# Gate matrices by one float32r matmul of 256 columns, and the entry to the second block by half features without GpSimd

## Chip, cores and metric

One core of a Trainium2 chip runs the kernel. The metric is device time in microseconds, the median of the timed runs. The engines are TensorE (PE; its weight loads are the row PEld), VectorE (DVE), ScalarE (ACT), GpSimd (POOL) and SyncE (SP), which issues most transfers.

## The reference

256 tokens of 1024 features pass two blocks. The first has a mixer (retention and differential attention) and then a retrieval feed-forward layer, the part that the change touches first:

```python
def peer_ffn(h, w_query, sub_keys, expert_u, expert_v):
    ...
        q = (hb @ w_query).reshape(t, PEER_HEADS, 2, PEER_HALF)
        s = jnp.einsum('thpc,hpnc->thpn', q, sub_keys).astype(jnp.float32)
        v1, i1 = lax.top_k(s[:, :, 0], PEER_TOPK)
        v2, i2 = lax.top_k(s[:, :, 1], PEER_TOPK)
        ...
        best, pos = lax.top_k(cand, PEER_TOPK)
        experts = jnp.take_along_axis(cand_idx, pos, axis=-1)
        gate = jax.nn.softmax(best, axis=-1).astype(hb.dtype)
        act = jax.nn.gelu(jnp.einsum('thkd,td->thk', u, hb), approximate=False)
        return jnp.einsum('thk,thkd->td', gate * act, vsel)
```

Eight heads pick 16 of 128 x 128 experts for each token. The second block has two layers. Each ends in attention to 256 memory tokens and a gated feed-forward layer; the first begins with a short convolution, the second with causal attention (`moba`) on rotated queries and keys:

```python
def short_conv_mixer(h, w_in, w_conv, w_out):
    b_gate, c_gate, u = jnp.split(h @ w_in, 3, axis=-1)
    z = c_gate * u
    conv = lax.conv_general_dilated(
    ...
    return (b_gate * conv) @ w_out
```

Everything is float32.

## The kernel before

**Weights.** A weight block of 128 x 1024 comes from memory into `raw` (three buffers). ScalarE rounds it to float32r (`whi`, three buffers), and VectorE or GpSimd, by `lo_plan`, subtracts to get the rest (`wlo`, two buffers). `block` multiplies it in three passes of eight matmuls of 256 columns: `whi` by the high part of the activations, `wlo` by the high part, `whi` by the low part.

**The expert layer** treats all experts densely. Each of 128 weight blocks of `peer_u` makes one chunk of 128 experts for 256 tokens, and `slots` holds [128, chunk, token]. The gate of a token is a 128 x 128 matrix, made by one matmul of two one-hot matrices over the 128 chosen (head, rank) pairs: `ohA` marks the second index, `ohB` the first one and holds the gate as its value. `group` does this for four tokens, and `hot` makes the one-hots two tokens at a time. From block 32 on a table spreads the 64 groups over the remaining 94 blocks (after one block, then after two, and so on), so a group meets chunks that are already there (`done` of them, which it multiplies on the spot) and others that are yet to come (it stores the gate, and the later gelu multiplies it in). The same tokens of successive chunks lie 1 KB apart in `slots`.

```python
                    for i in range(2):
                        nc.tensor.matmul(o[:, 2 * j + i], A[:, i], Bt[:, i], start=True, stop=True)
                sl = slots[:, :, ts].rearrange("p c t -> p t c")
                if done:
                    nc.vector.tensor_mul(sl[:, :, :done], o[:, :, :done], sl[:, :, :done])
                if done < NCH:
                    nc.scalar.copy(sl[:, :, done:], o[:, :, done:])
```

Then 128 blocks of `peer_v` multiply `slots` into two accumulators `acc[th]`, one for each half of the tokens; `product` adds a chunk to one, `collect` copies one out, transposes it and adds it to the residual `x`.

**The entry to the second block.** `conv_mixer` scales `x` into the parts `hh` and `hl`, squares and adds its eight feature slices (`track`: `accsq`, `acc`) for the norm, and runs eight steps `m`, each with a pair of blocks `o` (the inputs to z) and one block `b`. The results wait in PSUM for the norm `nr`; `gate` then makes z, convolves it, and multiplies by `b` into `ct`. PSUM has two tiles `sc` (for `o` of the first two steps) and three tiles `mm`. At step 1 a hook loads the keys and values of the first memory attention (`kvt`), which ScalarE rounds and GpSimd subtracts. Steps of the second memory's projection (`fill`, with `memx`, `hmh`, `hml`) are interleaved by the table `PLACES`.

A scheduler at build time fixes the order of each engine's queue.

Of the kernel before, what the change touches and what calls it, by code (L numbers as in the profile page):

```python
# [15 lines left out]
F32 = mybir.dt.float32  # L16
# [24 lines left out]
PLACES = {0: 1, 3: 1, 5: 2, 6: 1, 10: 1, 12: 1, 's': 2, 'h': 4, 'g': 10, 'n': 1, ('g', 0): 1, 'v': 4, ('d', 1): 1, ('o', 0): 3, ('o', 2): 1, ('o', 3): 1, ('o', 4): 1, ('o', 5): 4, ('o', 7): 10, ('c', 1): 1, ('c', 3): 1, ('c', 5): 1, 'ce': 1, 'm0': 1, 'mq0': 1, 'me0': 1, 'f0': 1, 'b': 2, 'bk': 1, 'bq': 1, ('mh0', 2): 1, ('bh', 0): 1, ('bh', 5): 1, ('bh', 7): 1}  # L41
# [5 lines left out]
GPLAN = "p"  # L47
HOT = 4
QSTEPS, USTEPS = 2, 4
HOOK = 1  # L50
# [6 lines left out]
CADD = 'vector'  # L57
MIXLO = 'v'
RETLO = 'v'
AHEAD = 3  # L60
# [11 lines left out]
class Build:  # L72
    def __init__(self, ctx, tc, io):
        self.ctx, self.tc, self.nc, self.io = ctx, tc, tc.nc, io
        self.const = ctx.enter_context(tc.tile_pool(name="const", bufs=1))
        self.wpool = ctx.enter_context(tc.tile_pool(name="weights", bufs=2))
        self.psfill = ctx.enter_context(tc.tile_pool(name="psfill", bufs=1, space=PSUM))
        self.lo_turn = 0
        self.folding = []
        self.filler = self.steady = iter(())  # L80
        self.rate, self.due = RATE, 0
        self.adder = self.nc.gpsimd
        self.lo_plan = "v"
# [628 lines left out]
    def peer(self):  # L712
        nc, io = self.nc, self.io
        with ExitStack() as ctx:
# [4 lines left out]
            h = self.placed(pool, "h2h", 48), self.placed(pool, "h2l", 48)  # L719
# [16 lines left out]
            selT = gpool.tile([P, 3, T], F32, name="selT")  # L736
# [215 lines left out]
            def product(c, th, a, b, w):  # L952
                tsl = slice(th * P, th * P + P)
                for s, (x, wt) in enumerate(((a, w[0]), (b, w[0]), (a, w[1]))):
                    for dh in range(2):
# [3 lines left out]
            def collect(th):  # L959

                tsl = slice(th * P, th * P + P)
                for q in range(4):
                    e = nc.scalar.copy if th or q % 2 else nc.vector.tensor_copy
                    e(ot[:, th, q * T:(q + 1) * T], acc[th][:, q // 2, q % 2 * T:q % 2 * T + T])
                for q in range(2):
                    tr = self.psum([P, 4, P])
                    for i in range(4):
                        k = 4 * q + i
                        nc.tensor.transpose(tr[:, i], ot[:, th, k * P:(k + 1) * P], self.ident)
                    for i in range(4):  # L970
                        k = 4 * q + i
                        nc.vector.scalar_tensor_tensor(self.x[:, k, tsl], tr[:, i], gate[:, k:k + 1],
                                                       self.x[:, k, tsl], op0=OP.mult, op1=OP.add)
# [12 lines left out]
            for c, parts in ends:  # L986
                product(c, 0, *parts)
            product(ends[0][0], 1, *ends[0][1])
            collect(0)
            product(ends[1][0], 1, *ends[1][1])  # L990
            collect(1)


    def mem_kv(self, pool, mpool, l, key, value, norm=None):
# [17 lines left out]
        for m2 in range(4):  # L1012
            o = self.psum([P, 2, T], "fill")
            for i in range(2):
                self.block(o[:, i], io["mem_wk"][l, 2 * m2 + i], hm, lo=FILL_LO, late=m2 == i == 0,
# [7 lines left out]
                if i == 1:  # L1023
# [4 lines left out]
                                      lambda n, i, o: value(n, o, rn), FILL_LO)  # L1028
# [47 lines left out]
    def mem_load(self, pool, l):  # L1076
# [3 lines left out]
        def load():  # L1080
            for n in range(4):
                for part in range(2):
# [5 lines left out]
                    nc.gpsimd.tensor_sub(lo, t, hi)  # L1088

        return (kT, v), load  # L1090

    def mem_fill(self, pool, mpool, l):
# [3 lines left out]
        def key(n, o, r):  # L1096
            t = mpool.tile([P, 2, T], F32, name="kvt", tag="kvt", bufs=1)
            hi, lo = (x[:, 2 * n:2 * n + 2] for x in kT)
            self.key_out(t, o, r)
            nc.scalar.copy(hi, t)  # L1100
            nc.gpsimd.tensor_sub(lo, t, hi)
# [125 lines left out]
    def conv_mixer(self, hook):  # L1227
        nc, io = self.nc, self.io
        with ExitStack() as ctx:
# [5 lines left out]
            def gate(m, o, b):  # L1235
                cu = pool.tile([P, 2, T], F32, name="cu", tag="cu", bufs=2)
# [9 lines left out]
                nc.gpsimd.tensor_mul(y, y, r)  # L1246
# [5 lines left out]
            self.adder = getattr(nc, CADD)  # L1252
            for k in range(KC):
                self.track(self.x[:, k], k)
            self.adder = nc.gpsimd
            for m in range(KC):
                self.at(("c", m))
                if m == HOOK:
                    hook()
                o = self.psum([P, 2, T], "sc" if m < 2 else "mm")  # L1260
                for i, c in enumerate((1, 2)):
                    self.block(o[:, i], io["conv_wi"][8 * c + m], h, late=m == i == 0)
                    if m == 1 and i == NORM1:
                        r = self.tracked_norm(pool, "nr", tables=True)
                b = self.psum([P, T])
# [78 lines left out]
    def moba(self):  # L1344
        nc, io = self.nc, self.io
        with ExitStack() as ctx:
            pool = self.pool(ctx, "moba")
            mask = self.load(pool, "causal", [P, 2, T])
            hk = self.gained(pool, self.x, G_KV)
            v = pool.tile([P, 2, 1024], F32, name="v")  # L1350
# [5 lines left out]
            def value(n, i, o):  # L1356
# [3 lines left out]
                if n == 1:  # L1360
                    rn = self.by_partition(pool, r, "aux")
                waiting.append((n, o))
# [8 lines left out]
            def plain(block, h, scale):  # L1371
                o = self.psum([P, T])
                self.block(o, block, h)
                t = pool.tile([P, T], F32, name="qkt", tag="qkt", bufs=3)
                nc.vector.scalar_tensor_tensor(t, o, scale, r, op0=OP.mult, op1=OP.mult)
                return t

            def rope(out, t):
                self.rope_out(pool, t, out, self.pcos, self.psin)
# [4 lines left out]
            hq = [self.placed(pool, "hq" + c, 32) for c in "hl"]  # L1384

            def query(hd):
                return plain(io["moba_wq"][hd], hq, 128.0 ** -0.5)
# [5 lines left out]
            for hd in range(KC):  # L1393
                t = plain(io["w_k"][hd], hk, 1.0)
# [3 lines left out]
                self.gain_chunk(self.x[:, hd], G_MIX + 1, hd, hq[0][:, hd], hq[1][:, hd])  # L1398
# [224 lines left out]
```

## Time and profile before

| | before |
|---|---|
| median of 3 runs | 1889.74 us (1888.1 to 1890.78) |
| profiled execution | 1882.41 us |
| its span in the trace | 1880.6 us |
| granted TensorE clock, mean | 0.992 |
| TensorE busy | 1833.2 us, 97% |
| VectorE, ScalarE, GpSimd busy | 1313.8, 975.1, 453.7 us |

The profiled execution is 1.8 us longer than its span and is one execution; sums in the text are made against it. Busy shares are averages over all stages, and matmuls overlap, so a stage has to be read by itself.

### The profile page before, as it was taken

How to read it: one execution, taken by the hardware profiler on the slowest of the kernel's cores; microseconds unless marked ns; L12 is line 12 of the kernel's file. 1: busy time of each engine (PE TensorE's matmuls, PEld its weight loads, DVE VectorE, ACT ScalarE, POOL GpSimd, SP SyncE). 2: the span in 40 equal slices, each digit the busy share in tenths (PEclk: the TensorE clock that was granted, in tenths of full speed). 3: DMA queues.
4: the chain of work that ended last, by engine and by line, in shares of the span. 5: the costliest groups of instructions: out<-in, count | busy, mean ns of one | idle time of the engine just before them, and what ended most of it. 6: DMA issues, size and time to landing. Idle time of an engine off the chain costs nothing.

```text
span 1880.6 us, 34809 instructions
## 1 busy us (share of the span) xinstructions
PE 1833.2 (97%) x13562; PEld 1717.2 (91%) x13562; DVE 1313.8 (70%) x2592; ACT 975.1 (52%) x1533; POOL 453.7 (24%) x254
## 2 busy tenths in 40 slices
PE   8999999999999999999999998999999999999997
PEld 6796888999999999788888878999999999999997
DVE  7879875995566676865555568777765679766654
ACT  7746335445555444445545555465554645555543
POOL 0001105787766777100000004112000111110001
PEclk9999999999999999999999999999999999999999
DMA  8763444454444444755555555544555553445553
GB/s 298 254 217 105 142 129 156 170 189 169 150 160 154 157 157 157 247 191 195 195 191 193 196 192 184 191 169 148 200 193 196 190 180 124 169 136 190 187 184 124
DMA packets 99765, 335.13 MB, mean 178 GB/s; under 512 B 12400, under 2 KB 13456, under 8 KB 99216
## 3 DMA queue, kind: packets, MB, share of 16 engines
q1 hardware_dynamic: 98160, 330.68, 51.0%
q8 instruction: 106, 1.74, 0.4%
q10 hardware_dynamic: 1440, 2.23, 0.3%
q14 instruction: 59, 0.48, 0.1%
HBM read 329.59 MB, written 3.28 MB: 177 GB/s over the span
## 4 chain that ended last, share of the span: by engine, by line
PE 87%; DVE 6%; DMA 3%; ACT 3%; issue 1%; POOL 0%; SPq 0%; DVEq 0%; ACTq 0%; POOLq 0%
PE mm L144 54%; PE pair L956 17%; PE mm L179 4%; PE pair L893 3%; PE fill L179 2%; DVE wlo L122 2%; PE fill L144 1%; PE sc L144 1%; DMA mraw<-w_mod 1%; PE aux L144 1%; DMA raw<-w_mod 1%; ACT whi L118 1%; DMA raw<-peer_v 0%; PE sc L628 0%; PE sc L554 0%
## 5 line engine op out<-in xcount | busy, mean ns | idle before, releaser
L118 ACT CAST whi<-raw 128x1024 fp32r<-128x1024 f32 x564 | 591.9, 1051 | 558.3 <-PE mm L144 280.4
L122 DVE TENSOR_TENSOR wlo<-raw,whi 128x1024 fp32r<-128x1024 f32 x420 | 526.7, 1255 | 298.7 <-PE pair L956 131.6
L122 POOL TENSOR_TENSOR wlo<-raw,whi 128x1024 fp32r<-128x1024 f32 x144 | 344.7, 2395 | 131.6 <-PE mm L144 113.6
L144 PE MATMUL mm<-hh,whi 128*128 128x256 f32 (+1 forms) x1184 | 178.2, 287 | 5.9 <-DVE ct L1248 5.1
L144 PE MATMUL mm<-hl,whi 128*128 128x256 f32 (+1 forms) x1184 | 174.5, 284 | 2.1 <-DVE hl L261 1.2
L144 PE MATMUL mm<-hh,wlo 128*128 128x256 f32 (+1 forms) x1184 | 175.9, 285 | 0.0
L144 PE MATMUL mm<-h2h,whi 128*128 128x256 f32 x1152 | 168.2, 289 | 4.1 <-ACT h2h L260 4.0
L226 POOL TENSOR_TENSOR acc<-acc,accsq 128x256 f32<-128x256 f32 x42 | 42.1, 1004 | 523.1 <-ACT accsq L224 523.1
L144 PEld LDWEIGHTS mm<-hh,whi 128*128 128x128 f32 x1184 | 155.4, 190 | 10.9 <-issue 7.6
L956 PE MATMUL pair<-whi,actl 128*128 128x512 f32 x512 | 158.6, 391 | 2.4 <-DVE actl L949 2.3
L956 PE MATMUL pair<-whi,acth 128*128 128x512 f32 x512 | 158.3, 390 | 0.3 <-ACT acth L948 0.2
L956 PE MATMUL pair<-wlo,acth 128*128 128x512 f32 x512 | 157.8, 389 | 0.7 <-DVE wlo L122 0.7
L144 PEld LDWEIGHTS mm<-hl,whi 128*128 128x128 f32 x1184 | 153.5, 189 | 5.0 <-DVE hl L261 1.7
L144 PEld LDWEIGHTS mm<-hh,wlo 128*128 128x128 f32 x1184 | 154.6, 190 | 3.5 <-issue 1.5
L144 PE MATMUL mm<-h2h,wlo 128*128 128x256 f32 x1152 | 157.5, 279 | 0.0
L144 PE MATMUL mm<-h2l,whi 128*128 128x256 f32 x1152 | 157.1, 279 | 0.0
L144 PEld LDWEIGHTS mm<-h2h,whi 128*128 128x128 f32 x1152 | 147.4, 192 | 5.0 <-ACT h2h L260 4.8
L144 PEld LDWEIGHTS mm<-h2h,wlo 128*128 128x128 f32 x1152 | 144.6, 189 | 0.0
L144 PEld LDWEIGHTS mm<-h2l,whi 128*128 128x128 f32 x1152 | 144.0, 189 | 0.0
L956 PEld LDWEIGHTS pair<-whi,actl 128*128 128x128 f32 x512 | 95.4, 188 | 24.4 <-DVE actl L949 5.0
L956 PEld LDWEIGHTS pair<-wlo,acth 128*128 128x128 f32 x512 | 96.0, 188 | 21.3 <-DVE wlo L122 1.1
L956 PEld LDWEIGHTS pair<-whi,acth 128*128 128x128 f32 x512 | 95.5, 188 | 20.9 <-ACT acth L948 1.5
(407 smaller groups left out, 3062.7 us busy)
## 6 DMA issues: line engine op xcount, KB each, us to landing
raw<-peer_u SPq DMA_DIRECT2D x128, 512.0 KB, 3.5
raw<-peer_v SPq DMA_DIRECT2D x128, 512.0 KB, 3.5
raw<-ffn_gu SPq DMA_DIRECT2D x88, 512.0 KB, 4.3
raw<-ffn_dn SPq DMA_DIRECT2D x44, 512.0 KB, 3.9
raw<-w_mod SPq DMA_DIRECT2D x64, 256.0 KB, 3.8
raw<-conv_wi SPq DMA_DIRECT2D x24, 512.0 KB, 3.5
raw<-mem_wk SPq DMA_DIRECT2D x16, 512.0 KB, 4.5
mraw<-w_mod SPq DMA_DIRECT2D x16, 512.0 KB, 6.2
```

Source lines behind the costliest of these rows:

```text
L118: self.hi_copy = nc.scalar.copy(hi, raw)
L122: (nc.vector if plan == "v" else nc.gpsimd).tensor_sub(lo, raw, hi)
L144: self.matmul = nc.tensor.matmul(out, a, b, start=first and j == 0, stop=last and j == 3 * n - 1)
L179: self.matmul = nc.tensor.matmul(outs[i // 2][:, i % 2], a[:, k, :], b[:, w], start=k == 0 and s == 0 and i % 2 == 0, stop=k == 7 and s == ...
L226: self.adder.tensor_add(self.acc, self.acc, self.last)
L893: nc.tensor.matmul(o[:, 2 * j + i], A[:, i], Bt[:, i], start=True, stop=True)
L956: nc.tensor.matmul(acc[th][:, dh], x[:, tsl], wt[:, dh * 512:dh * 512 + 512], start=c == 0 and s == 0, stop=c == NCH - 1 and s == 2)
```

## The change

In the gates, `ohA` and `ohB` become float32r, and `ohB` has two halves of 128 columns: one holds the gate rounded to float32r, the other the rounded rest (the first times `gate_ratio`, made by ScalarE). One matmul of 256 columns makes both products. ScalarE copies the second from PSUM into `glo`, VectorE adds the first, and for the finished chunks GpSimd multiplies into `slots`. `GPLAN` gives every fourth `wlo` of the stage to VectorE; the one-hot buffers go from four to three and are made two ahead instead of three.

At the end of the expert layer the last products and `collect` go by half features, so that features 0 to 511 of both token halves come out first; the first convolution block takes its eight feature slices in two halves (`late=4`). From there on no addition, subtraction or gate operation of the second block is left to GpSimd: `acc`, memory parts, z and the rope product move to VectorE (a scaling of the convolution to ScalarE). The hook starts at step 3 and gives two pieces a step, two `fill` places go, and `moba` folds the norm into cosine and sine.

```diff
@@ constants
-PLACES = {..., ('c', 1): 1, ('c', 3): 1, ('c', 5): 1, ...}
+PLACES = {..., ('c', 5): 1, ...}
...
-GPLAN = "p"
-HOT = 4
+GPLAN = "ppvp"
+HOT = 3
...
-HOOK = 1
+HOOK = 3
...
-AHEAD = 3
+AHEAD = 2
...
-        self.adder = self.nc.gpsimd
+        self.adder = self.nc.vector
@@ def mm3
-            order.sort(key=lambda si: (si[1], si[0]))
+            order.sort(key=lambda si: (si[1] // int(late), si[0], si[1]))
@@ turn, in peer
-                    nc.scalar.copy(selT[:, :, cols], tr)
+                    nc.scalar.copy(selT[:, :, cols], tr[:, 0:2])
+                    hi, ratio = gate_hi[:, cols], gate_ratio[:, cols]
+                    nc.scalar.copy(hi.bitcast(F32R), tr[:, 2])
...
+                    nc.vector.tensor_mul(ratio, low, inv)
@@ hot, in peer
-                    A = gpool.tile([P, 2, P], F32, name="ohA", tag="ohA", bufs=HOT)
-                    Bt = gpool.tile([P, 2, P], F32, name="ohB", tag="ohB", bufs=HOT)
+                    A = gpool.tile([P, 2, P], F32R, name="ohA", tag="ohA", bufs=HOT)
+                    Bt = gpool.tile([P, 2, 2, P], F32R, name="ohB", tag="ohB", bufs=HOT)
                     t = g * TG + 2 * j
+                    for i in range(2):
+                        nc.vector.tensor_scalar(Bt[:, i, 0], iota, selT[:, 0, t + i:t + i + 1],
+                                                gate_hi[:, t + i:t + i + 1], op0=OP.is_equal, op1=OP.mult)
+                        nc.scalar.activation(Bt[:, i, 1], Bt[:, i, 0].bitcast(F32), AF.Copy,
+                                             scale=gate_ratio[:, t + i:t + i + 1])
...
-                    for i in range(2):
-                        nc.vector.tensor_scalar(Bt[:, i], iota, selT[:, 0, t + i:t + i + 1],
-                                                selT[:, 2, t + i:t + i + 1], op0=OP.is_equal, op1=OP.mult)
@@ group, in peer
-                o = self.psum([P, TG, P], "pair")
+                o = self.psum([P, TG, 2, P], "pair")
...
+                lo = gpool.tile([P, TG, P], F32, name="glo", tag="glo", bufs=2)
+                nc.scalar.copy(lo, o[:, :, 1])
                 sl = slots[:, :, ts].rearrange("p c t -> p t c")
                 if done:
-                    nc.vector.tensor_mul(sl[:, :, :done], o[:, :, :done], sl[:, :, :done])
+                    nc.vector.tensor_add(lo[:, :, :done], o[:, :, 0, :done], lo[:, :, :done])
+                    nc.gpsimd.tensor_mul(sl[:, :, :done], lo[:, :, :done], sl[:, :, :done])
                 if done < NCH:
-                    nc.scalar.copy(sl[:, :, done:], o[:, :, done:])
+                    nc.vector.tensor_add(sl[:, :, done:], o[:, :, 0, done:], lo[:, :, done:])
@@ end of peer
-            for c, parts in ends:
-                product(c, 0, *parts)
-            product(ends[0][0], 1, *ends[0][1])
-            collect(0)
-            product(ends[1][0], 1, *ends[1][1])
-            collect(1)
+            waiting = None
+            for dh in range(2):
+                for th in range(2):
+                    for c, parts in ends:
+                        product(c, th, *parts, halves=(dh,))
+                    if waiting:
+                        collect(*waiting)
+                    waiting = th, dh
+            collect(*waiting)
@@ mem_load
-                    nc.gpsimd.tensor_sub(lo, t, hi)
+                    nc.vector.tensor_sub(lo, t, hi)
+                    yield
@@ gate, in conv_mixer
-                nc.vector.tensor_mul(cu, o, r[:, None, :].to_broadcast([P, 2, T]))
...
-                nc.gpsimd.tensor_mul(z, cu[:, 0], cu[:, 1])
+                nc.vector.tensor_mul(z, o[:, 0], r2)
+                nc.vector.tensor_mul(z, o[:, 1], z)
...
-                nc.vector.tensor_scalar(y, z, cw[:, m, 2:3], None, op0=OP.mult)
+                nc.scalar.activation(y, z, AF.Copy, scale=cw[:, m, 2:3])
...
-                nc.gpsimd.tensor_mul(y, y, r)
+                nc.vector.tensor_mul(y, y, r)
@@ conv_mixer
-                if m == HOOK:
-                    hook()
+                if m >= HOOK:
+                    for _ in range(2):
+                        next(hook, None)
```

The order of the queues moves at three places. The first is TensorE's queue in the gate stage, before (`pair` is the group's PSUM tile, `h2h` and `h2l` the activations):

```order
L893 MATMUL pair<-ohB,ohA 128x128 x4
L144 MATMUL mm<-h2h,whi 128x256 x8
L144 MATMUL mm<-h2h,wlo 128x256 x8
L144 MATMUL mm<-h2l,whi 128x256 x8
L893 MATMUL pair<-ohB,ohA 128x128 x4
```

And after:

```order
L902 MATMUL pair<-ohB,ohA 128x256 x4
L143 MATMUL mm<-h2h,whi 128x256 x8
L143 MATMUL mm<-h2h,wlo 128x256 x8
L143 MATMUL mm<-h2l,whi 128x256 x8
L902 MATMUL pair<-ohB,ohA 128x256 x4
```

The groups stand where they stood; a group is still four matmul instructions, now of 256 columns. (In the trace before, each float32 matmul leaves two records.)

The second place is GpSimd's queue. Before, the whole expert layer reads:

```order
L226 TENSOR_TENSOR acc<-acc,accsq 128x256 x6
L122 TENSOR_TENSOR wlo<-raw,whi 128x1024 x144
L1088 TENSOR_TENSOR memk0l<-kvt,memk0h 128x512
L1088 TENSOR_TENSOR memv0l<-kvt,memv0h 128x2x256
L234 TENSOR_TENSOR acc<-acc,accsq 128x256
```

After, late in the gate stage:

```order
L121 TENSOR_TENSOR wlo<-raw,whi 128x1024
L908 TENSOR_TENSOR slots<-glo,slots 128x4x108
L908 TENSOR_TENSOR slots<-glo,slots 128x4x110
L121 TENSOR_TENSOR wlo<-raw,whi 128x1024 x2
L908 TENSOR_TENSOR slots<-glo,slots 128x4x112
L121 TENSOR_TENSOR wlo<-raw,whi 128x1024
L908 TENSOR_TENSOR slots<-glo,slots 128x4x112
```

Between the `wlo` there now stand products into `slots`, in places two in a row, and fewer `wlo`.

The third place is VectorE's queue at the entry, from the last additions of squares to the norm, before:

```order
L226 TENSOR_TENSOR acc<-acc,accsq 128x256
L275 SCALAR_TENSOR_TENSOR hml<-memx,gains,hmh 128x256
L226 TENSOR_TENSOR acc<-acc,accsq 128x256
L275 SCALAR_TENSOR_TENSOR hml<-memx,gains,hmh 128x256 x4
L122 TENSOR_TENSOR wlo<-raw,whi 128x1024 x3
L202 TENSOR_SCALAR nra<-aux 128x256
L122 TENSOR_TENSOR wlo<-raw,whi 128x1024
L211 SCALAR_TENSOR_TENSOR nra<-nra,nry 128x256
```

And after:

```order
L225 TENSOR_TENSOR acc<-acc,accsq 128x256
L1101 TENSOR_TENSOR memk0l<-kvt,memk0h 128x512
L225 TENSOR_TENSOR acc<-acc,accsq 128x256
L121 TENSOR_TENSOR wlo<-raw,whi 128x1024
L225 TENSOR_TENSOR acc<-acc,accsq 128x256
L1101 TENSOR_TENSOR memv0l<-kvt,memv0h 128x2x256
L225 TENSOR_TENSOR acc<-acc,accsq 128x256
L121 TENSOR_TENSOR wlo<-raw,whi 128x1024
L225 TENSOR_TENSOR acc<-acc,accsq 128x256
L274 SCALAR_TENSOR_TENSOR hml<-memx,gains,hmh 128x256
```

The `wlo` no longer stand behind all of the `hml`, and the subtractions of the memory parts (`memk0l`, `memv0l`) stand among them.

## Rows read from the trace of the kernel before

**Rows 1.** The page: span, two engines (busy, share, instructions), the chain by engine.
```profile
span 1880.6 us, 34809 instructions
...
PE 1833.2 (97%) x13562; PEld 1717.2 (91%) x13562; DVE 1313.8 (70%) x2592; ACT 975.1 (52%) x1533; POOL 453.7 (24%) x254
...
PE 87%; DVE 6%; DMA 3%; ACT 3%; issue 1%; POOL 0%; SPq 0%; DVEq 0%; ACTq 0%; POOLq 0%
```

**Rows 2.** Busy time by stretch, gate stage: PE, PEld, DVE, ACT, POOL, clock, DMA.
```profile
443.00:751.00 308.00, 308.00 (x2680) 308.00 (x2679) 190.34 (x481) 153.08 (x246) 217.22 (x92) 1.00 0.45 156
```

**Rows 3.** The chain that ended last, gate stage: start, length, what.
```profile
609.02 5.66 PE mm L144 x48
614.67 0.89 PE pair L893 x8
615.57 2.74 PE mm L144 x24
618.31 0.89 PE pair L893 x8
619.20 5.66 PE mm L144 x48
```

**Rows 4.** Groups by shape, 443 to 751 us: count, busy us, mean ns, idle before.
```profile
L122 POOL TENSOR_TENSOR wlo<-raw,whi 128x1024 fp32r<-128x1024 f32 x92 | 219.9, 2390 | 90.9 <-PE mm L144 87.9 <-ACT slots L898 2.9
...
L877 DVE TENSOR_TENSOR ohA<-fill,selT 128x256 f32<-128x256 f32 x124 | 51.9, 418 | 84.1 <-PE pair L893 83.9
...
L896 DVE TENSOR_TENSOR slots<-pair,slots 128x472 f32<-128x472 f32 x2 | 2.5, 1264 | 0.0
...
L898 ACT COPY slots<-pair 128x376 f32<-128x376 f32 x2 | 1.7, 842 | 0.9 <-DVE slots L896 0.9
...
L896 DVE TENSOR_TENSOR slots<-pair,slots 128x136 f32<-128x136 f32 x2 | 0.9, 452 | 0.4 <-PE pair L893 0.4
...
L898 ACT COPY slots<-pair 128x152 f32<-128x152 f32 x2 | 0.9, 438 | 1.6 <-DVE slots L896 1.6
```

**Rows 5.** Groups by shape, whole span, same columns.
```profile
L118 ACT CAST whi<-raw 128x1024 fp32r<-128x1024 f32 x564 | 591.9, 1051 | 558.3 <-PE mm L144 280.4 <-PE pair L956 145.4 <-DMA raw<-peer_v 31.9
L122 DVE TENSOR_TENSOR wlo<-raw,whi 128x1024 fp32r<-128x1024 f32 x420 | 526.7, 1255 | 298.7 <-PE pair L956 131.6 <-ACT whi L118 69.6 <-PE mm L144 43.0
...
L1294 ACT CAST fh<-fs 128x256 fp32r<-128x256 f32 x44 | 17.9, 407 | 21.2 <-DVE fs L1293 21.1
```

**Rows 6.** Timeline of POOL: start, length, operation, [idle before, releaser].
```profile
1172.65 0.73 POOL L1239 TENSOR_TENSOR z<-cu 128x256 f32<-128x256 f32 x1 [6.63 <-DVE cu L1237]
...
1239.70 3.38 POOL L1101 TENSOR_TENSOR memk1l<-kvt,memk1h 128x512 fp32r<-128x512 f32 x1 [2.91 <-ACT memk1h L1100]
1276.60 1.29 POOL L1101 TENSOR_TENSOR memk1l<-kvt,memk1h 128x512 fp32r<-128x512 f32 x1 [33.52 <-ACT memk1h L1100]
```

**Rows 7.** The chain at the entry to the second block.
```profile
1118.71 0.65 PE pair L956 x3
...
1123.95 0.47 PE sc L144 x2
...
1158.65 4.59 PE mm L144 x24
```

**Rows 8.** Timeline at the entry.
```profile
1123.77 3.24 DVE L275 SCALAR_TENSOR_TENSOR hl<-x,gains,hh 128x256 fp32r<-128x256 f32 x8
...
1130.30 0.48 DVE L275 SCALAR_TENSOR_TENSOR hml<-memx,gains,hmh 128x256 fp32r<-128x256 f32 x1
...
1138.69 2.08 PE L144 MATMUL sc<-hh,wlo 128*128 128x256 f32 x8 [3.29 <-DVE wlo L122]
...
1158.65 1.90 PE L144 MATMUL mm<-hh,whi 128*128 128x256 f32 x8 [5.11 <-DVE ct L1248]
```

**Rows 9.** Busy time by stretch at the entry, columns as in rows 2.
```profile
1124.00:1129.00 5.00, 5.00 (x30) 5.00 (x31) 3.54 (x10) 5.00 (x15) 0.00 (x0) 0.66 0.93 310
...
1159.00:1166.00 7.00, 7.00 (x49) 7.00 (x48) 5.94 (x9) 2.35 (x3) 3.12 (x3) 0.77 0.33 115
```

More of the change, by code (lines that the diff above doesn't have):

```diff
@@ L735, in peer @@
             sel = [take(3 * P).rearrange("p (a n) -> p a n", a=3) for _ in range(2)]
-            selT = gpool.tile([P, 3, T], F32, name="selT")
+            selT = gpool.tile([P, 2, T], F32, name="selT")
+            gate_hi, gate_ratio = gpool.tile([P, T], F32, name="gatehi"), self.r0
             qs = [take(T) for _ in range(4)]
@@ L950, in chunk, with product, collect @@
                 return a, b, w
-            def product(c, th, a, b, w):
+            def product(c, th, a, b, w, halves=range(2)):
                 tsl = slice(th * P, th * P + P)
                 for s, (x, wt) in enumerate(((a, w[0]), (b, w[0]), (a, w[1]))):
-                    for dh in range(2):
+                    for dh in halves:
                         nc.tensor.matmul(acc[th][:, dh], x[:, tsl], wt[:, dh * 512:dh * 512 + 512],
                                          start=c == 0 and s == 0, stop=c == NCH - 1 and s == 2)
-            def collect(th):
+            def collect(th, dh):
                 tsl = slice(th * P, th * P + P)
[L962 to L973, printed above, removed]
+                for q, e in zip((2 * dh, 2 * dh + 1), (nc.scalar.copy, nc.vector.tensor_copy)):
+                    e(ot[:, th, q * T:(q + 1) * T], acc[th][:, dh, q % 2 * T:q % 2 * T + T])
+                tr = self.psum([P, 4, P])
+                for i in range(4):
+                    k = 4 * dh + i
+                    nc.tensor.transpose(tr[:, i], ot[:, th, k * P:(k + 1) * P], self.ident)
+                for i in range(4):
+                    k = 4 * dh + i
+                    nc.vector.scalar_tensor_tensor(self.x[:, k, tsl], tr[:, i], gate[:, k:k + 1],
+                                                   self.x[:, k, tsl], op0=OP.mult, op1=OP.add)
             gate = self.mod[:, 40:48, 0]
@@ L1014, in mem_kv @@
             for i in range(2):
-                self.block(o[:, i], io["mem_wk"][l, 2 * m2 + i], hm, lo=FILL_LO, late=m2 == i == 0,
+                self.block(o[:, i], io["mem_wk"][l, 2 * m2 + i], hm, lo="v" if l else FILL_LO, late=m2 == i == 0,
                            w=first if l == m2 == i == 0 else None)
@@ L1087, in load @@
                     nc.scalar.copy(hi, t)
-                    nc.gpsimd.tensor_sub(lo, t, hi)
-        return (kT, v), load
+                    nc.vector.tensor_sub(lo, t, hi)
+                    yield
+        return (kT, v), load()
     def mem_fill(self, pool, mpool, l):
@@ L1250, in gate @@
                 nc.vector.tensor_sub(cat[1][:, m], t, cat[0][:, m])
-            self.adder = getattr(nc, CADD)
+            self.adder = nc.vector
             for k in range(KC):
                 self.track(self.x[:, k], k)
-            self.adder = nc.gpsimd
             for m in range(KC):
                 self.at(("c", m))
-                if m == HOOK:
-                    hook()
+                if m >= HOOK:
+                    for _ in range(2):
+                        next(hook, None)
                 o = self.psum([P, 2, T], "sc" if m < 2 else "mm")
                 for i, c in enumerate((1, 2)):
-                    self.block(o[:, i], io["conv_wi"][8 * c + m], h, late=m == i == 0)
+                    self.block(o[:, i], io["conv_wi"][8 * c + m], h, late=4 if m == i == 0 else 0)
                     if m == 1 and i == NORM1:
                         r = self.tracked_norm(pool, "nr", tables=True)
+                        r2 = pool.tile([P, T], F32, name="r2")
+                        nc.vector.tensor_mul(r2, r, r)
                 b = self.psum([P, T])
@@ L1349, in moba @@
             hk = self.gained(pool, self.x, G_KV)
+            nc.vector.tensor_scalar(self.gains[:, G_MIX + 1], self.gains[:, G_MIX + 1], 128.0 ** -0.5, None,
+                                    op0=OP.mult)
+            hq = [self.placed(pool, "hq" + c, 40) for c in "hl"]
+            cosr, sinr = (pool.tile([P, T], F32, name=n) for n in ("cosr", "sinr"))
             v = pool.tile([P, 2, 1024], F32, name="v")
@@ L1361, in value @@
                     rn = self.by_partition(pool, r, "aux")
+                    nc.vector.tensor_mul(cosr, self.pcos, r)
+                    nc.vector.tensor_mul(sinr, self.psin, r)
+                for k in (2 * n, 2 * n + 1):
+                    self.gain_chunk(self.x[:, k], G_MIX + 1, k, hq[0][:, k], hq[1][:, k])
                 waiting.append((n, o))
@@ L1369, in moba, with plain, rope @@
             self.natural("mm", [io["w_v"][q] for q in range(8)], toks, value)
-            def plain(block, h, scale):
+            def plain(block, h):
                 o = self.psum([P, T])
                 self.block(o, block, h)
[L1374 to L1379, printed above, removed]
+                return o
+            def rope(out, o):
+                t = pool.tile([P, T], F32, name="roper", tag="roper", bufs=2)
+                nc.vector.stream_shuffle(t, o, [(i + 16) % 32 for i in range(32)])
+                nc.vector.tensor_mul(out, o, cosr)
+                nc.vector.tensor_mul(t, t, sinr)
+                nc.vector.tensor_add(out, out, t)
                 return out
@@ L1383, in moba @@
             kT = pool.tile([P, KC, T], F32, name="k")
-            hq = [self.placed(pool, "hq" + c, 32) for c in "hl"]
             def query(hd):
-                return plain(io["moba_wq"][hd], hq, 128.0 ** -0.5)
+                return plain(io["moba_wq"][hd], hq)
             def turned(t):
```

17 lines of the change are left out of this document (9 added, 8 removed).

## Prediction

> **What bounds the kernel now.** I read the page first: TensorE works in 97% of the span, and of the chain that ended last it holds 87%, so a change is worth what it takes from TensorE's own work or from TensorE's waits [rows 1]. Then I read the busy time by stretch. In the gate stage (443 to 751 us) TensorE and its weight loads are busy in all 308 us, with VectorE at 190, ScalarE at 153 and GpSimd at 217 us beside them [rows 2]. No helper ends last there; only fewer or shorter matmuls help. The chain through that stage shows its rhythm: two blocks, a group of gates, one block, a group, and so on [rows 3]. A period of three blocks and two groups takes 10.18 us (609.02 to 619.20): 5.66 + 0.89 + 2.74 + 0.89.
>
> The entry to the second block is the opposite case. The chain's piece of expert products ends at 1118.71 + 0.65 = 1119.36 and the first convolution matmul starts at 1123.95 [rows 7]. The timeline then shows TensorE idle for 3.29 us before 1138.69 on a `wlo` of VectorE, and for 5.11 us before 1158.65 on `ct` of VectorE [rows 8]. The last wait is one for a PSUM tile: the third output block `b` needs the tile that `ct` of the first frees. [...]
>
> **Gates on TensorE.** Before, a group of four tokens is eight float32 records in 0.89 us [rows 3]. After, it is four float32r matmuls of 256 columns. Float32r matmuls of 256 columns are what the weight blocks are made of: 24 in 2.74 us or 48 in 5.66, 0.114 to 0.118 us each [rows 3], so a group should take 0.457 to 0.472; I take 0.465. That saves 0.425 us in each of 64 groups: **27.2 us** (bounds 26.8 and 27.7). A period of 10.18 becomes 9.33 us and the stage about 281 us.
>
> **What the helpers get for it.** They need to stay under 281 us.
> ScalarE loses 62 copies into `slots` of about 199 elements, 0.52 us each by the slope between 842 ns at 376 elements and 438 at 152 [rows 4], 32 us. It gets 256 scalings of 128 elements and 64 copies of 512. Contiguous casts took 407 ns at 256 elements and 1051 at 1024 [rows 5], which makes 0.30 us at 128 and 0.62 at 512, 77 and 40 us. Sum 153 - 32 + 117 = 238 us, 85%.
> VectorE loses 63 strided products of 313 elements on average, 0.88 us each by the slope between 1264 ns at 472 and 452 at 136 (55 us), and gets 64 adds of 313 elements on average into a contiguous tile (0.48 each by the slope between 418 ns at 256 and 1255 at 1024, 31 us), 62 strided adds of about 199 elements (0.60 by the slope of the strided product, 37 us), and 23 of the 92 `wlo` (1.23 each, 28 us) [rows 4, 5]. Sum 190 - 55 + 96 = 231 us, 82%.
> GpSimd keeps 71 of the 94 `wlo` that stand from the first group on in the order: 71 times 2.39 is 170 us [rows 4]. It gets 64 products of 4x32 to 4x124 elements, 20,040 in all, which read and write `slots` with a step of 1 KB. No row has a strided GpSimd operation. Contiguous ones took 0.73 us at 256 elements, 1.29 at 512 and 2.39 at 1024 [rows 4, 6]: 0.17 us and 2.17 ns an element, the lower bound, 54 us in all. On the other engines the step costs something on top: ScalarE 1.80 ns an element strided against 0.84 contiguous, VectorE 2.42 against 1.09, so 1.0 and 1.3 ns more [rows 4, 5]; as a ratio VectorE's 2.2 would make 4.8 ns on GpSimd, the upper bound, 107 us. I take the added nanoseconds, since GpSimd's slope is already the longest and the step touches the same memory: 3.4 ns, **79 us**. Sum 249 us, 89%. The last periods decide: 2.25 `wlo` (5.38) and two products of 496 elements (1.86 each) are 9.10 us of 9.33. It fits, barely; at 4.8 ns it stops fitting at 94 finished chunks, and the last 22 groups lose 0.29 us each on average, 6 us.
> [...]
>
> **Do the waits in line bite?** In ScalarE's queue the second scaling for a group stands right behind the copy of the group before, and the next group comes at least one block (2.74 us) later, so copy (0.62), scaling (2 x 0.3) and a cast of a weight in front (1.05) fit. In GpSimd's queue two products stand between two `wlo` once in two periods; that `wlo` then has a few tenths to spare near the end. VectorE and GpSimd also hold each other up: the same 512-element subtraction took 1.29 us at one place and 3.38 at another, where VectorE worked beside it [rows 6]. The 23 `wlo` on VectorE read two SBUF tensors, as those operations did. At about 1 us each that is 20 us more for VectorE (about 251, still under 281) and about 10 for GpSimd. I take **2.5 us** of it as seen by TensorE (bounds 0 and 14, the 6 above and 8 for the holds). Gates: 27.2 - 2.5 = 24.7 us.
>
> **The entry.** By the order of VectorE's queue, from the last product to the first `ct` stand: a copy, four `x`, eight `hl`, seven adds, eight `wlo`, four subtractions of 512, seven `hml`, six short norm and `r2` operations, and 4 + 4 + 2 + 1 for the first two gates. An `hl` took 3.24 / 8 us, an `hml` 0.48 [rows 8], the others go by elements as above: 0.4 + 1.1 + 3.2 + 2.9 + 9.8 + 2.8 + 3.4 + 2.1 + 1.7 + 1.9 + 0.8 + 0.4 = 30.5 us [rows 4, 5], and the four `x` wait some 1 to 1.5 us for the transposes, the third `wlo` about 1 us for a cast of ScalarE that stands behind `kvt` from memory: 33 us. Before, the third `b` block started 39.3 us after the last product (1158.65 - 1119.36) [rows 7]. I take **6.2 us** off. The 3.29 us wait should vanish, since `wlo` of the fourth block stands behind two adds and one subtraction and no longer behind eight `hml` with GpSimd between; the wait for `ct` stays, at some 5 us, and with it one stretch at the lower clock. Bounds: nothing, if ScalarE's casts or the weight transfers end last instead; and 10, if both waits and one clock dip go (3.29 + 5.11 + 1.85, the last being 4.59 - 2.74 for a block). Product by halves asks for the last chunk's operands some 0.6 us earlier, which the 512-column matmuls before it can hide or not; it is inside these bounds.
>
> **The rest.** 48 adds of the running norm leave GpSimd for VectorE, 0.42 us each, 20 us on an engine that is idle 30% of the span [rows 1, 4]; rope loses a hop over GpSimd at the same number of VectorE operations; two memory-key steps come later, same work. I take 0.6 us off (between -2 and +2).
>
> **Sum.** 24.7 + 6.2 + 0.6 = 31.5 us off the profiled execution's 1882.4 (span 1880.6 and 1.8 around it): 1850.9. The three timed runs have a median of 1889.74, 0.4% above that execution; scaled, the forecast is **1858 us**.
>
> **Rivals.** (1) GpSimd or VectorE becomes the bound late in the gate stage: strided products near 4.8 ns and holds on the `wlo` cost the full 14 us, 1872. For it: 89% load, queues in order. Against: before, GpSimd's `wlo` stayed at 2.39 us with VectorE busy three fifths of the stage [rows 2, 4]. [...] (2) The entry gains nothing, since VectorE does by itself what two engines did: 1864. (3) The other side: a GpSimd product costs more than 6.7 ns an element. Then 170 + 11 + 134 us reach 315, which is the old stage and the entry's gain; at 8 ns it is 341 us, 33 more than before, and the kernel takes about 1916. No row comes near that price. (4) The gate matmul of 256 columns costs as much as two float32 records; then only the entry is left, about 1884. Against it stand the weight blocks' matmuls of that shape [rows 3].
>
> **How the numbers follow.** This forecast 0.58, (1) 0.18, (2) 0.11, (3) 0.08, (4) 0.05. Its own range is 1850 to 1865 (best bounds 27.7 + 10 + 2). For 8 in 10 I take 1848 to 1877, which holds the forecast, (1) and (2). About 0.2% (4 us) is what a measurement of this kernel can tell from no change. Faster: 0.58 + 0.18 + 0.11 and 0.01 of (4), 0.88; the rest of (4) is the same, 0.04; slower is (3), 0.08.
>
> **What would show it.** The stage between first and last group near 281 us with TensorE at 100%; a group at 0.46 us in the chain; GpSimd's product at about 1.9 us for 496 elements and its `wlo` no longer waiting on TensorE; no wait for `wlo` at the entry and one for `ct` that ends some 33 us after the last product. TensorE waiting on GpSimd's `wlo` late in the stage would make it wrong, as would a group that still takes 0.89.

## The result, and the profile after

The changed kernel takes 1862.9 us in the median (1854.8 to 1864.8) against 1890.1 for the one before (four runs each; a fifth run of the changed kernel, 1868.9 us, is not in that median): ratio 0.9858, 95% interval 0.9825 to 0.9891, so 27 us or 1.4% faster. The forecast was 1858.0. The profiled execution is the fastest of its runs, 1854.8 us, 27.6 below the profiled execution of before.

The page after, first the span and the engines, then the chain by engine and by line, beside [rows 1]:

```profile
span 1853.0 us, 34715 instructions
...
PE 1806.6 (97%) x13306; PEld 1689.2 (91%) x13306; DVE 1358.1 (73%) x2762; ACT 1051.6 (57%) x1797; POOL 378.3 (20%) x202
...
PE 87%; DVE 6%; ACT 3%; DMA 2%; issue 1%; POOL 1%; SPq 0%; DVEq 0%; ACTq 0%; POOLq 0%
```

TensorE still ends nearly everything. Its busy time fell by 26.6 us; its idle time, span less busy, hardly moved (47.4 to 46.4). That little change hides a loss and a gain that nearly cancel, and the rest of this section looks for both.

The chain in an undisturbed piece of the gate stage (start, length, what), beside [rows 3]:

```profile
500.12 0.47 PE pair L902 x4
500.59 5.65 PE mm L143 x48
506.24 0.47 PE pair L902 x4
506.71 2.74 PE mm L143 x24
509.45 0.47 PE pair L902 x4
```

A group takes 0.47 instead of 0.89 us and a period 9.33 instead of 10.18. In 64 groups that is 26.9 us. Yet from the first to the last group it is 294.5 us (440.5 to 735.0) after 312.8 (441.4 to 754.2), 18.3 less. The 8.6 us that are missing stand in two views. First TensorE's two largest waits from 440 to 744 us (what it waited for, total us, times, longest); the kernel before had none from its first group to its last:

```profile
PE mm L143 <- DVE wlo L121: 3.7, 1, 3.7
PE pair L902 <- ACT ohB L887: 2.8, 2, 1.5
```

And the windows at the stage's start (columns as in [rows 2]):

```profile
440.50:463.20 22.70, 16.94 (x117) 15.77 (x118) 18.35 (x43) 13.90 (x33) 10.68 (x8) 0.85 0.32 110
463.20:500.00 36.80, 36.80 (x318) 36.80 (x317) 29.14 (x75) 29.02 (x64) 26.64 (x18) 1.00 0.48 171
```

In the first 23 us TensorE stood idle for 5.8 us. The granted clock averages 0.85 there, and 0.52 from 450.48 to 454.22: in that piece, behind the longest wait, 16 matmuls took 3.74 us in the chain where 1.83 is usual (two thirds of the 2.74 above), 1.9 us more. With a later wait of 1.5 us near 609 us that is 9.2 us, a little over the 8.6. From 463 to 585 and from 611 us to the stage's end TensorE doesn't wait at all.

The long wait in detail, one row each from the timelines of TensorE, VectorE and GpSimd (start, length, engine, operation, in brackets the idle time before it and its releaser):

```profile
450.48 2.07 PE L143 MATMUL mm<-h2h,wlo 128*128 128x256 f32 x8 [3.73 <-DVE wlo L121]
...
447.07 3.35 DVE L121 TENSOR_TENSOR wlo<-raw,whi 128x1024 fp32r<-128x1024 f32 x1
...
447.00 2.34 POOL L121 TENSOR_TENSOR wlo<-raw,whi 128x1024 fp32r<-128x1024 f32 x1
```

VectorE's first subtraction of the stage begins 0.07 us after one of GpSimd and takes 3.35 us instead of 1.25 [rows 5]: it ends 1.1 us after GpSimd's, which took 2.34. In VectorE's queue it stands behind the new ratios and five pairs of one-hots. TensorE was idle from 446.75, so without the 2.1 us of the hold these rows would still leave a wait of some 1.6 us.

At the entry, TensorE's and VectorE's rows in the order in which the wait forms:

```profile
1100.73 0.39 PE L968 MATMUL pair<-wlo,acth 128*128 128x512 f32 x1
1100.96 0.38 PE L979 MATMUL mm<-ident,slots 128*128 128x128 f32 x2
...
1106.04 1.20 PE L143 MATMUL sc<-hh,whi 128*128 128x256 f32 x4 [1.82 <-ACT hh L273]
...
1131.54 0.74 DVE L1261 TENSOR_TENSOR ct<-mm,cy 128x256 f32<-128x256 f32 x2
...
1132.10 1.15 PE L143 MATMUL mm<-hh,whi 128*128 128x256 f32 x8 [1.61 <-DVE ct L1261]
```

The last product gives way to a transpose at 1100.96, the third `b` starts at 1132.10: 31.1 us, where it was 39.3. The wait for `wlo` (3.29 us before) is gone; the one for `ct` is 1.61 instead of 5.11 [rows 8], with no lower clock behind it (1.00 from 1132.10 to 1134.84; eight matmuls in 1.15 us, where it was 1.90).

| stretch | before, us | after, us | change | forecast |
|---|---|---|---|---|
| start to first group | 441.4 | 440.5 | -0.9 | 0 |
| first to last group | 312.8 | 294.5 | -18.3 | -24.7 |
| last group to last product | 365.2 | 366.0 | +0.8 | 0 |
| last product to third `b` | 39.3 | 31.1 | -8.2 | -6.2 |
| third `b` to end | 721.9 | 720.9 | -1.0 | -0.6 |

These are single executions. A second one of the changed kernel (`after_again`, below) has 442.0, 294.8, 367.2, 31.2 and 727.0 us for the five stretches. The two that carry the gain repeat within 0.3 us; the others move by 1.2 to 6.1, so their small changes show nothing.

### The profile page after: what moved, and what is told of

The parts are those of the page before. It is cut to its first block, busy times and chain, and to the rows that moved or that the text cites. A ratio compares the mean times of both kernels' runs of the same rounds, so it can differ in the third digit from the quotient of the medians.

```text
span 1853.0 us, 34715 instructions
## 1 busy us (share of the span) xinstructions
PE 1806.6 (97%) x13306; PEld 1689.2 (91%) x13306; DVE 1358.1 (73%) x2762; ACT 1051.6 (57%) x1797; POOL 378.3 (20%) x202
## 4 chain that ended last, share of the span: by engine, by line
PE 87%; DVE 6%; ACT 3%; DMA 2%; issue 1%; POOL 1%; SPq 0%; DVEq 0%; ACTq 0%; POOLq 0%
PE mm L143 54%; PE pair L968 18%; PE mm L178 4%; PE fill L143 2%; PE fill L178 2%; PE pair L902 1%; DVE wlo L121 1%; ACT whi L117 1%; PE aux L143 1%; PE mm L323 1%; PE sc L143 1%; POOL wlo L121 1%; DMA raw<-w_mod 1%; POOL slots L908 0%; DMA mraw<-w_mod 0%
## 5 line engine op out<-in xcount | busy, mean ns | idle before, releaser
L121 DVE TENSOR_TENSOR wlo<-raw,whi 128x1024 fp32r<-128x1024 f32 x444 | 553.3, 1247 | 268.1 <-PE pair L968 127.0
L121 POOL TENSOR_TENSOR wlo<-raw,whi 128x1024 fp32r<-128x1024 f32 x120 | 289.8, 2421 | 133.5 <-PE mm L143 121.0
L143 PE MATMUL mm<-h2h,whi 128*128 128x256 f32 x1152 | 161.4, 283 | 4.5 <-ACT h2h L259 4.0
L885 DVE TENSOR_SCALAR ohB<-fill,selT,gatehi 128x128 fp32r<-128x128 f32 x256 | 96.1, 399 | 31.9 <-PE pair L902 31.7
```

What stands on the lines that cost most here:

```text
L121: (nc.vector if plan == "v" else nc.gpsimd).tensor_sub(lo, raw, hi)
L885: nc.vector.tensor_scalar(Bt[:, i, 0], iota, selT[:, 0, t + i:t + i + 1], gate_hi[:, t + i:t + i + 1], op0=OP.is_equal, op1=OP.mult)
```

## Experiments

Ratios are to the kernel before, with 95% intervals.

**The two parts alone.** `gates_alone` keeps the old entry, `entry_alone` the old gates (the constants are put in one line here):

```diff
-GPLAN, HOT, AHEAD, HOOK = "p", 4, 3, 1
+GPLAN, HOT, AHEAD, HOOK = "ppvp", 3, 2, 1    # gates_alone, with turn, hot and group as changed
+GPLAN, HOT, AHEAD, HOOK = "p", 4, 3, 3       # entry_alone, with all else as changed
```

> The kernel before with the gate part of the change alone (float32r one-hots, 256 columns, every fourth subtraction of the stage on VectorE). By the ledger of the two profiled executions (gate stage 312.8 to 294.8 us between first and last group, 1.0 us won just ahead of it) this part gives 19 us: 1871, ratio 0.990. Rival: the two parts aren't independent and the entry gains only because of the gates; then this part alone gives the whole 27 us, 1863, and the entry alone nothing.

> The kernel before with everything but the gate part. By the ledger the time from the last expert product to the third output block b of the convolution falls by 8.2 us and the rest by 0.5: about 1881, ratio 0.9955, with no wait of TensorE for wlo at the entry and one for ct under 2 us, where the forecast let it stay at some 5. The prediction's own figure was 6.2 and 0.6, 1883. Rival: no gain by itself, 1890.

The gates alone: 1871.3 us, 0.9907 (0.9879 to 0.9935). The entry alone: 1880.6 us, 0.9960 (0.9941 to 0.9979). In the median of the kernel before beside them (1888.7), 17.4 and 8.1 us: they add up to 25.5 beside the change's 27, so within the scatter the parts are independent, and both gain. The stretches agree: from first to last group it is 294.6 us with the gates alone and 312.8 with the entry alone; from the last product to the third `b` it is 31.5 us with the entry alone, where the wait for `ct` is 2.1 us, a little over the 2 expected. TensorE's idle time says it too: 47.4 us before, 55.5 with the gates alone (+8.1), 41.0 with the entry alone (-6.4). The gates alone keep the 3.7 us wait for `wlo` at the stage's start and both old waits of the entry:

```profile
PE mm L144 <- DVE ct L1261: 4.7, 1, 4.7
...
PE mm L144 <- DVE wlo L122: 3.7, 1, 3.7
PE sc L144 <- DVE wlo L122: 3.3, 1, 3.3
```

**Who is late at the start of the gate stage.**

```diff
-                self.lo_plan = UPLAN if cp < R1 else GPLAN
+                self.lo_plan = UPLAN if cp < R1 + 8 else GPLAN   # late_vector
-GPLAN = "ppvp"
+GPLAN = "p"                                                      # all_pool
```

> The changed kernel, but VectorE gets its share of the subtractions only from chunk pair 24 on (GpSimd makes all of the first 16 blocks of the gate stage, where its products are short). Theory A: the 7.7 us that TensorE loses in the first 23 us of the stage come from VectorE being late there, 2.1 us of it because its first subtraction is held behind GpSimd's (3.35 us instead of 1.25). Then the wait of TensorE for that wlo (3.7 us) falls under 1 us and the time by 3 to 5 us. Rival C: the new ratio work (3.4 us on VectorE ahead of the first one-hots) alone makes it late and the subtraction is innocent: the waits at the start stay at 5 to 6 us and the time stays. Rival D: GpSimd can't carry 16 blocks alone and TensorE waits for its wlo instead: slower by 3 us or more.

> The changed kernel with every subtraction of the gate stage on GpSimd. GpSimd's load would be 94 x 2.43 + 74 (64 products at 0.27 us and 2.82 ns an element, as measured) = 302 us, over the 295 of the stage. Theory A: the start of the stage gets shorter by 3 to 5 us as with the late share, but the end of the stage waits for GpSimd's wlo by some 8 to 12 us: 1866 to 1872. [...]

`late_vector`: 1859.2 us, 0.9838 (0.9814 to 0.9861). `all_pool`: 1865.5 us, 0.9874 (0.9852 to 0.9897). The same window of `late_vector` as above:

```profile
440.50:463.20 22.70, 21.37 (x178) 20.89 (x177) 21.18 (x57) 18.00 (x42) 17.82 (x12) 1.00 0.48 155
```

And TensorE's waits in its stage:

```profile
PE pair L902 <- ACT ohB L887: 1.5, 1, 1.5
PE pair L902 <- DVE ohA L889: 1.3, 2, 0.9
```

The wait for `wlo` and the lower clock are gone (1.00 for 0.85), and from first to last group it is 286.6 us (445.0 to 731.6), 7.9 less; 0.9 us of that comes back as a wait for `ohA` just ahead of the first group. In the median the run is 3.7 us below the changed kernel, as Theory A said, but the two intervals overlap. Rival D has nothing for it. The run takes four of VectorE's 24 subtractions away, with their own work and their place in its queue, so it shows what VectorE's share costs at the start and not the hold by itself. In `all_pool` the stage is 289.6 us (443.5 to 733.1): the start is repaired too, and only at its end does GpSimd, full from 580 us on, let TensorE wait for `wlo` (2.8 us). The expert products then start 12.7 us after the last group, and 8.8 in `late_vector`: another 4. So GpSimd can carry nearly all of the subtractions, and the end costs about 7 us, a little less than expected.

```diff
+                if cp == R1 + 8:
+                    finish(gate_hi[:, P:], gate_ratio[:, P:])   # defer_ratio: max, reciprocal, product
```

> The changed kernel, but the ratio of the second 128 tokens is finished only at chunk pair 24 (those tokens come into groups 32 and up), which takes 1.4 us of VectorE from ahead of the first one-hots. Rival C (the ratio work makes VectorE late at the start): TensorE's waits at the start, 3.7 for wlo and 1.3 for ohB, fall by 1 to 2 us. Theory A (the subtraction that stands on VectorE so early, and its hold behind GpSimd's, is the cause): they stay within 0.5 us, and so does the time, 1863 within the scatter.

1865.9 us, 0.9894 (0.9853 to 0.9936), and the waits stay:

```profile
PE mm L143 <- DVE wlo L121: 3.5, 1, 3.5
...
PE pair L906 <- ACT ohB L891: 2.6, 3, 1.5
...
PE pair L906 <- DVE ohA L893: 1.1, 1, 1.1
```

This put off only the ratio of the second 128 tokens, 1.4 us. VectorE's first subtraction then begins 11.2 us after its first ratio operation, where it was 11.5: the time goes into a longer wait for ScalarE's `glo` (1.38 us for 0.55). So as far as it was tested Rival C falls, and Theory A stands. Another rival was not tested by itself: the change also makes the one-hots two ahead instead of three, and the waits of 1.5 and 1.3 us for `ohB` and `ohA` that are left in `late_vector` may come from that.

**The products back on VectorE.**

```diff
-GPLAN = "ppvp"
+GPLAN = "p"
-                    nc.gpsimd.tensor_mul(sl[:, :, :done], lo[:, :, :done], sl[:, :, :done])
+                    nc.vector.tensor_mul(sl[:, :, :done], lo[:, :, :done], sl[:, :, :done])
```

> The changed kernel with all subtractions of the gate stage on GpSimd and the 64 products on VectorE instead: the load is 228 us on GpSimd and about 235 - 24 x 1.6 + 56 = 253 on VectorE, both under the 286 us that TensorE needs. Theory A and the ledger: no early subtraction on VectorE and GpSimd not the bound, so TensorE's waits in the stage fall from 7.3 us to under 3, and the time by 4 to 7 us against the changed kernel, 1856 to 1859. Rival: the products on VectorE stand ahead of the one-hots in its queue, TensorE waits for ohA and ohB in each period, and the gain is gone: 1866 or more.

1876.8 us, 0.9945 (0.9923 to 0.9967): 14 us slower than the change, and the rival is right. The stage's groups of the products and of the scalings:

```profile
L908 DVE TENSOR_TENSOR slots<-glo,slots 128x128 f32<-128x128 f32 (+31 forms) x64 | 103.2, 1613 | 0.0
...
L887 ACT ACTIVATE ohB<-ohB,r 128x128 fp32r<-128x128 f32 x256 | 90.6, 397 | 67.2 <-DVE ohB L885 67.1
```

I had priced a product at 0.88 us, as it was when it read PSUM and `slots` [rows 4]; reading `glo` and `slots` beside GpSimd's subtractions it takes 1.61 on average (the two of 384 elements took 1.41 and 2.73). The one-hots stand behind it, ScalarE waits 67 us for them ahead of the scalings (26 in the changed kernel), and TensorE waits 13 times for `ohB` (9.0 us).

**The entry.**

```diff
-                    nc.vector.tensor_sub(lo, t, hi)
+                    nc.gpsimd.tensor_sub(lo, t, hi)   # mem_gpsimd, in mem_load
-            for dh in range(2):
-                for th in range(2):
+            for th in range(2):                       # token_halves, with late=True for late=4
+                for dh in range(2):
```

> The changed kernel with the eight subtractions of the memory keys and values at the entry back on GpSimd (the rest of the entry as changed). Theory E (GpSimd's operations hold VectorE's up): eight operations of 0.68 us go from VectorE, 5.4 us or about 3 of them ahead of ct, but VectorE's additions and wlo beside GpSimd's 1.3 to 2.3 us get longer by 0.5 to 1 us each, and the wait for ct stays or grows: 1.6 us becomes 1.5 to 4. Rival F (VectorE's own work is the limit, the holds are nothing): ct comes 3 us earlier, its wait vanishes, time 1 to 2 us less.

> The changed kernel with the last expert products and collect by token halves again, and the first convolution block by single feature slices as before. The time from the last product to the first convolution matmul was 4.6 us before and 4.9 after, so the half features give nothing there by the ledger: the same time within 1.5 us, TensorE's idle time at the collect unchanged at 3 to 4 us. Rival: they do give the early start of hl and the additions, and without them the entry loses 2 to 3 us.

`mem_gpsimd`: 1867.0 us, 0.9897 (0.9856 to 0.9939). A wait of 2.17 us for a `wlo` comes back at 1132.87 and the one for `ct` is 2.63 us, though VectorE has less to do. VectorE's rows show why (the same additions into `cy` took 0.87 us in pairs in the changed kernel):

```profile
1132.74 1.92 DVE L1255 SCALAR_TENSOR_TENSOR cy<-z,conv_w,cy 128x255 f32<-128x255 f32 x2
1134.58 1.88 DVE L1257 SCALAR_TENSOR_TENSOR cy<-z,conv_w,cy 128x254 f32<-128x254 f32 x2
...
1132.88 1.49 POOL L1101 TENSOR_TENSOR memv0l<-kvt,memv0h 128x512 fp32r<-128x512 f32 x1 [3.21 <-ACT memv0h L1100]
1134.32 1.46 POOL L1101 TENSOR_TENSOR memk0l<-kvt,memk0h 128x512 fp32r<-128x512 f32 x1
```

Each of the two pairs is 1.0 us longer, beside an operation of GpSimd that runs at the same time. Theory E holds, rival F falls: eight short subtractions on GpSimd cost TensorE 3.2 us of waits.

`token_halves`: 1864.8 us, 0.9897 (0.9852 to 0.9942), idle time 47.9 us against 46.4, with 1.1 us more of waits at the collect (1.22 and 1.65 for `slots`, where the changed kernel has 0.27 and 1.51) and 0.4 more for `ct`. That is at the edge of the expectation: the half features are worth some 1.5 us of waits, which the times don't resolve.

**The changed kernel again, and a later share for VectorE.**

```diff
-                self.lo_plan = UPLAN if cp < R1 else GPLAN
+                self.lo_plan = UPLAN if cp < R1 + 20 else GPLAN   # later_vector; latest_vector: R1 + 28
```

> The changed kernel itself once more, for its scatter: with the two profiled executions so far 8 us under their medians at equal idle time of TensorE, the difference between executions should lie in TensorE's busy time (1806.6 us there, 1813 to 1818 in the other kernels with the same 13306 matmuls), not in its waits. Expected: median 1860 to 1865, idle time 46 to 47 us, busy time 1807 to 1818, and the same 3.7 us wait for wlo at the start of the gate stage.

> The changed kernel, VectorE's share of the subtractions only from chunk pair 36 on. With all of them on GpSimd, TensorE had no wait from 463 to 660 us and GpSimd was full from 580 us on; with VectorE's share from pair 24 on one wait of 1.5 us for ohB stayed at 606 us, behind a transfer that waited for a GpSimd subtraction held to 3.4 us. Theory A: starting at about 565 us takes that hold's damage away too: stage 284 to 286 us from first to last group (294.8 changed, 286.9 with the share from pair 24 on), waits in it under 1.5 us, 1856 to 1859. Rival: two subtractions at once hold each other wherever the share starts, the wait only moves: 2 to 3 us of waits, 1858 to 1861.

> The changed kernel, VectorE's share of the subtractions only from chunk pair 44 on, which is behind the place (two groups with one block between) where the share from 24 and from 36 on both left one wait of 1.5 us for ohB: there a GpSimd subtraction took 3.35 us because one of VectorE began 0.36 us ahead of it, the buffer raw came free late, and ScalarE's cast and scalings stood behind the transfer. Theory A: without a VectorE subtraction at that place the wait goes, the waits of the stage fall from 2.8 to 1.3 us and the time to 1853 to 1856. Rival: GpSimd, full from 580 us on, has no room left, its subtractions come late between 600 and 700 us and TensorE waits 2 us or more for them: 1857 or more.

`after_again`: 1862.9 us, 0.9858 (0.9836 to 0.9880), with the same 3.73 us wait and 48.8 us idle, 2 more than expected. `later_vector`: 1855.7 us, 0.9816 (0.9793 to 0.9840), 286.7 us from first to last group (441.8 to 728.5). `latest_vector`: 1858.1 us, 0.9848 (0.9823 to 0.9873), 284.3 us (442.9 to 727.2). The wait of 1.5 us near 600 us, where two groups have only one block between them, stayed in the first, as its rival said, and went in the second. There, in `later_vector`, GpSimd's timeline has two subtractions, and the chain shows the first at 3.35 us and the transfer behind it:

```profile
592.97 5.73 POOL L121 TENSOR_TENSOR wlo<-raw,whi 128x1024 fp32r<-128x1024 f32 x2
...
593.01 3.35 POOL wlo L121
...
596.38 3.47 DMA raw<-peer_u
```

And two in a row in `latest_vector`, with none of VectorE's beside them:

```profile
587.46 4.78 POOL L121 TENSOR_TENSOR wlo<-raw,whi 128x1024 fp32r<-128x1024 f32 x2
```

So that wait comes from the hold, too, by way of a buffer: GpSimd's subtraction ends late, `raw` is free late, the transfer (3.47 us) lands late, and ScalarE's cast of it has the scalings behind it in line. The time of `latest_vector`, 1858.1, lies in its rival's range all the same, though the wait for GpSimd that the rival asked for isn't there (0.2 us). The times of the three versions with a late share (1859.2, 1855.7, 1858.1) can't be told apart; their idle times are 43.4, 43.0 and 42.2 us, where the changed kernel's two executions had 46.4 and 48.8. All three lie below the changed kernel, by 4 to 7 us in the median, with intervals that overlap its own; `later_vector` is the fastest that was run.

## Why the prediction was right

**Gates on TensorE, 27.2.** Right: 0.47 for 0.465 us a group, 26.9 us. Rival (4) is out. The stage of 281 us was counted from the window of 308, which leaves out 4.8 us of it: from first to last group before it is 312.8, and 27.2 less is 285.6. The three late versions took 284.3 to 286.7.

**The helpers.** From first to last group GpSimd was busy 237 us (249 expected), VectorE 235 (231, or 251 with holds) and ScalarE 229 (238). A product on GpSimd took 1.20 us on average (1.23 expected), and its rows give the slope that I had to bound:

```profile
L908 POOL TENSOR_TENSOR slots<-glo,slots 128x136 f32<-128x136 f32 x2 | 1.3, 656 | 2.0 <-DVE glo L907 2.0
...
L908 POOL TENSOR_TENSOR slots<-glo,slots 128x488 f32<-128x488 f32 x1 | 1.6, 1645 | 0.0
```

(1645 - 656) / (488 - 136) = 2.8 ns an element, between the lower bound of 2.17 and the 3.4 taken, far from the 6.7 of rival (3); a product of 488 elements took 1.65 us, where 1.9 was expected for 496. The added nanoseconds of the other engines were the wrong measure, though near enough. The 2.8 are 1.3 times the 2.17 of the contiguous operations of before [rows 4, 6]. The sum holds: the late end of the stage, where rival (1) saw GpSimd as the bound, has no wait (in `after_again` one of 1.0 us for GpSimd's `wlo`, behind the last group).

**Loss in the gate stage, 2.5.** This is the term that was mis-sized: 9.2 us (8.6 by the stretches), inside its bounds of 0 and 14, but in another place than those bounds were made of. I looked for it late in the stage, where the loads are highest, and priced holds as an average (1 us each, 20 in all). On average they were less: VectorE's 24 subtractions took 1.64 us instead of 1.25, 9 us in all, and between 463 and 609 us TensorE saw none of that. Most of the damage was done at the first one: a hold of 2.1 us is the larger part of a wait of 3.7, with a dip of the clock to 0.52 behind it. `late_vector` shows what the place costs: with VectorE's first four subtractions elsewhere, 7.9 us of the stage return. That it hurts there because nothing is made ahead yet, one-hots and `wlo` each being just in time, is my reading of the rows and no run's. The second hold that hurt, by way of the wait near 609 us, met a place where the groups stand closer.

Where the two engines' subtractions met at the stage's start, only one got longer: VectorE's took 3.35 us instead of 1.25, GpSimd's 2.34 beside 2.39 on average before [rows 4]. No other of VectorE's took that long: of the 24, 11 took 1.20 to 1.26 us, 12 took 1.43 to 2.45, and only the first 3.35.

**Entry, 6.2.** Right in kind, 8.2 in size. The count of VectorE's queue was 30.5 us of work and 2.5 of waiting, 33 to the third `b`; it was 31.1, with VectorE busy for 29.4 of 30.9 us. Both parts of the count were about 1 us too long. What failed beside it is the step that let the wait for `ct` stay at some 5 us, with a stretch at the lower clock (before, the block of 4.59 us behind that wait ran at 0.63 on average): it was 1.61, without one (1.00). Why VectorE gets through more in less time shows in the old entry: it was busy 34.9 of 39.2 us there, for 57 instructions, and now 29.4 for 62. `mem_gpsimd` shows that GpSimd's operations make the difference in part: its eight subtractions alone cost 3.2 us. Rival (2) is out by `entry_alone`.

**The rest, 0.6.** 1.0 after the entry, 0.9 won and 0.8 lost ahead of it: within the bounds, and within what two executions of one kernel differ by, so neither shown nor refuted.

**Sum.** 31.5 expected, 27.6 found between the profiled executions and 27.2 between the medians: 6.4 too much at the gates, 2.0 too little at the entry, 0.5 elsewhere. Errors of opposite sign partly cancel: that the total is off by only 3.9 us, where the gates are off by 6.4, is luck. The 4 us that the forecast took as measurable were too few: the interval of the ratio is 6 us wide to either side.

## What to carry to other kernels

Where two engines hold each other up, the mean cost of a hold said little here: ask where the waiting engine's result is needed at once. Try sharing work with a second engine only once the first one is full; the late versions that do so had 3 to 4 us less idle time than the profiled change and were 4 to 7 us below the change in the median, with intervals that overlap. When work is taken from an engine that holds another, count the holds in the old trace (durations of one operation, side by side) as part of the gain.

## What the hardware showed unasked

The same code runs in two paces at the same granted clock (1.00). Two executions of the changed kernel, the same stretches (PE busy and matmuls, clock, DMA), first the profiled one, then `after_again`:

```profile
350.00:400.00 50.00, 50.00 (x443) 1.00 0.55 190
1750.00:1800.00 50.00, 50.00 (x444) 1.00 0.53 190
```

```profile
350.00:400.00 50.00, 50.00 (x427) 1.00 0.57 183
1750.00:1800.00 50.00, 50.00 (x427) 1.00 0.56 185
```

TensorE starts 443 or 444 matmuls in 50 us, or 427: 0.113 or 0.117 us each, 4% apart, for a whole stretch. Which stretch has which pace changes between executions of one kernel. It goes with the scatter: with 13306 matmuls in each, the changed kernel's busy time was 1806.6 us in one execution and 1813.4 in the other, 6.8 of the 9.2 us between their spans. So two single executions can't be compared to better than some 8 us by their spans; their idle times agree to some 2 us (46.4 and 48.8), and the length of the long wait to 0.01 (3.73 in both). What sets the pace stays open: I found nothing in these traces that goes with it.
